# A norm's sums one unit later, single PSUM tiles at the start and in the last attention output, and seven products in one more column group

## The chip, the cores and the metric

One core of a Trainium2 chip runs the whole program in one launch. The metric is the device time of that launch in microseconds; the kernel before has a median of 2023.74 us in the three runs shown (2023.49 to 2025.34). The engines are TensorE (PE, with its weight loads PEld), VectorE (DVE), ScalarE (ACT), GpSimd (POOL) and SyncE (SP, which issues most transfers).

## The reference

A decoder of two layers over 256 tokens of width 2048. Layer 0 mixes by causal pooling, layer 1 by attention with keys and values computed from the stream after layer 0; each is followed by a gated FFN with a causal convolution. Every addition is followed by a layer norm.

```python
def layer_norm(x, g, b):
    mu = jnp.mean(xf, axis=-1, keepdims=True)
    var = jnp.mean(jnp.square(xf - mu), axis=-1, keepdims=True)
    y = (xf - mu) * lax.rsqrt(var + LN_EPS) * g + b
...
    for i in range(DEPTH):
        if i < N_A_LAYERS:
            mix = pool_mixer(h, pool_w_in[i], pool_w_grp[i], pool_scale[i], pool_w_out[i])
        else:
            if i == N_A_LAYERS:
                k_shared = (h @ shared_w_k).reshape(B_, S, N_HEADS, HEAD_DIM)
                v_shared = (h @ shared_w_v).reshape(B_, S, N_HEADS, HEAD_DIM)
            mix = dilated_attention(h, k_shared, v_shared, attn_w_q[j], attn_w_o[j])
        h = layer_norm(DEEPNORM_ALPHA * h + mix, ln1_g[i], ln1_b[i])
        ff = conv_ffn(h, ffn_w_up[i], ffn_conv_w[i], ffn_conv_b[i], ffn_w_down[i])
        h = layer_norm(DEEPNORM_ALPHA * h + ff, ln2_g[i], ln2_b[i])
    return h
```

## The kernel before

**Units.** All matrix products are cut into units: a block of 512 weight rows by 512 columns, loaded as one tile `raw`. A unit's float32 weights are split into a high part `wh` (cast by ACT, L99) and a low part `wl` (the rest, by DVE, L100), and three products of high and low parts stand for one float32 product. `run_units` walks through the list of units. For unit i it first calls `ahead(i)`, which issues loads up to five units on and splits up to three units on (`SP_AHEAD`); `wh` and `wl` have four buffers each, `raw` has three. Then come the functions that were put in `before[i]`, the unit's matmuls, then the functions in `pending` whose count has run out, and last the unit's own `post`. `later(n, fn)` puts a function in `pending`, to run n units on. Each engine carries out its instructions strictly in the order in which this walk writes them.

**Activations.** The stream stands transposed in four quarters `H[0..3]` (128 partitions x 4 x 256 tokens), with high and low parts for the matmuls in `XC[q]` (and in `XP[q]`, the stream scaled by the norm's gain but not yet normed). The start transposes x with TensorE into PSUM tiles `xT` (`x_quad`, L535 on): ACT casts the high part into XC, DVE subtracts for the low part, and ACT copies the float32 into H. PSUM has four tiles of two banks; `bank` gives one bank of such a tile, `pair` both.

**The norm.** `add_last` is the last product of a half layer. Behind its four column groups, `resid_last` adds the result to H, squares it, and folds it into the sums `S` and `Q`. `shift` first takes the mean of quarter 0 from all quarters, for quarters 1 to 3 of a second half layer (`first` false) by GpSimd transfers that accumulate (`less`, L409). `chain` (L428) lets TensorE sum S and Q over the partitions (L429, L430), and from these ACT and DVE make the reciprocal deviation and the mean; then come, a unit apart each, `norm(q)` (DVE, L443 and L444), `affine(q)` (ACT, L450, and the cast L452) and `lo(q)` (DVE, L305: the low part of XC[q]).

The first product after a norm does not wait for it: it uses XP and is corrected when it is evacuated (`norm_evac`, L474 to L478). After layer 0's FFN these are the four units of K for head group 0, called k0 to k3 here. The next four, q0 to q3, are Q for the same heads; q0 is the first to read XC[0], q3 the first to read XC[3]. Then come the units of V.

**Seven products.** Some units of the FFN's second product (`group_tm`, `mk_seven`) make a two by two block product with seven products of half size instead of eight; `sevens` says in which column groups. Such a unit is split in two, "a" and "b", and DVE forms sums of weight blocks for them (`split_sums`, L113 to L124). Quarters 0 to 6 of the first FFN do so in all four column groups, quarter 7 in two.

**Attention outputs.** `outputs(hq, ms)` multiplies the transposed weights with V for two heads at a time into one pair of banks; ACT casts the high part (L1119), DVE makes the low part (L1120). The product with `attn_w_o` follows, whose last unit of a column group reads these.

Of the kernel before, what the change touches and what calls it, by code (L numbers as in the profile page):

```python
# [9 lines left out]
F32 = mybir.dt.float32  # L10
# [3 lines left out]
OP = mybir.AluOpType  # L14
# [3 lines left out]
T = 256  # L18
P = 128
# [13 lines left out]
def trunk(ctx: ExitStack, tc: tile.TileContext, x, pool_w_in, pool_w_grp, pool_scale, pool_w_out,  # L33
# [3 lines left out]
    V, A, PE = nc.vector, nc.scalar, nc.tensor  # L37
# [10 lines left out]
    def pair(nm):  # L48
        return psp.tile([P, 2, 512], F32, name=nm, tag="ps")

    def bank(nm):
        return pair(nm)[:, 0, :]

    def pairs(ps, n=4):
        return [(m, min(2, n - m), ps[m].both) for m in range(0, n, 2)]
# [16 lines left out]
    pending, before = [], {}  # L72
# [62 lines left out]
    def later(n, fn):  # L135
        if n == 0:
            fn()
        else:
            pending.append([n, fn])
# [158 lines left out]
    def w4(nm):  # L298
        return lnp.tile([P, 4, T], F32, name=nm, tag="w4")

    def quad_tile(nm):
        return xcp.tile([P, 4, 2, XW], F32R, name=nm, tag="xc")

    def lo_part(dst, src, n):
        V.tensor_tensor(dst[:, 0:n, 1, :T], src, dst[:, 0:n, 0, :T].bitcast(F32), OP.subtract)  # L305
# [9 lines left out]
    H, XC, XP, ST = {}, {}, {}, {}  # L315
    vec, cvec, gbx = [], [], {}
    ident = const.tile([P, P], F32, name="ident")
# [13 lines left out]
    def resid_last(c, first, lay, which, after):  # L331
        def post(ps):
            for m, n, p in pairs(ps):
                y = H[c][:, m:m + n, :]
                if first and c == 0:
                    V.scalar_tensor_tensor(y, y, ALPHA, p[:, :, :T], op0=OP.mult, op1=OP.add)
                else:
                    V.tensor_tensor(y, y, p[:, :, :T], OP.add)
                if c < 3:
                    V.tensor_tensor(y, y, p[:, :, T:], OP.add)  # L340
                else:
                    square(3, m)
            if c == 0:
                ST["w4"] = w4("fold")
                s = fold(H[0], None, "S0", F32R)
                later(1, lambda: shift(s, first, lay, which))
            elif c < 3:
                n = 3 if c == 1 and not first else 1
                later(n, lambda: stats(c))
                later(n + 1, lambda: xp(c, lay, which))  # L350
            else:
                folds(3)
                xp(3, lay, which)
                later(1, lambda: chain(ps[0], lay, which, after))
        return post

    def square(q, m):
        if m == 0:
            ST["sq"] = lnp.tile([P, 4, T], F32, name="sq", tag="sq")
        A.activation(ST["sq"][:, m:m + 2], H[q][:, m:m + 2], AF.Square)  # L360
# [12 lines left out]
    def folds(q):  # L373
        ST["S"] = fold(H[q], ST["S"], "S")
        ST["Q"] = fold(ST["sq"], ST["Q"], "Q")

    def stats(q):
        square(q, 0)
        square(q, 2)
        folds(q)  # L380

    def shift(s, first, lay, which):
        ps = bank("shift")
        PE.matmul(ps[:, :T], ones4, s, start=True, stop=True)
        if first:
            cs = ST["w4"][:, 3:4, :]
        else:
            cs = pools["ffn"].tile([P, 2, T], F32, name="cs", tag="xs", bufs=1)[:, 0:1, :]
        A.activation(cs[:, 0, :], ps[:, :T], AF.Copy, scale=-1.0)
        cb = cs.to_broadcast([P, 4, T])  # L390
        ST["S"] = ST["Q"] = None

        def one():
            V.tensor_tensor(H[0], H[0], cb, OP.add)
            if first:
                pre(1)
            stats(0)

        def two():
            xp(0, lay, which)  # L400
            if first:
                pre(2)
                pre(3)

        def pre(q):
            V.scalar_tensor_tensor(H[q], H[q], ALPHA, cb, op0=OP.mult, op1=OP.add)

        def less(q):
            nc.gpsimd.dma_start(H[q], cb, accum_op=OP.add)  # L409

        later(1, one)
        later(2, two)
        if not first:
            for q in (1, 2, 3):
                less(q)

    def xp(q, lay, which):
# [10 lines left out]
    def chain(ps, lay, which, after):  # L428
        PE.matmul(ps[:, :T], onesd, ST["S"], start=True, stop=True)  # L429
        PE.matmul(ps[:, T:], onesd, ST["Q"], start=True, stop=True)  # L430
        rm = lnp.tile([P, 4, T], F32, name="rm", tag="sq")
        rs, mr, var = rm[:, 0, :], rm[:, 1, :], rm[:, 2, :]
        ST["rs"], ST["mr"] = rm[:, 0:1, :], mr
        A.activation(rm[:, 3, :], ps[:, :T], AF.Square)
        V.tensor_tensor(var, ps[:, T:], rm[:, 3, :], OP.subtract)
        A.activation(var, var, AF.Sqrt, bias=epst)
        V.reciprocal(rs, var)
        V.tensor_tensor(mr, ps[:, :T], rs, OP.mult)
        mb, rb = rm[:, 1:2, :].to_broadcast([P, 4, T]), rm[:, 0:1, :].to_broadcast([P, 4, T])
        g0 = 32 * which  # L440

        def norm(q):
            V.tensor_tensor(H[q], H[q], rb, OP.mult)  # L443
            V.tensor_tensor(H[q], H[q], mb, OP.subtract)  # L444

        def affine(q):
            XC[q] = quad_tile("xc")
            for m in range(4):
                j = 4 * q + m
                A.activation(H[q][:, m, :], H[q][:, m, :], AF.Identity,  # L450
                             scale=vec[lay][:, g0 + j:g0 + j + 1], bias=vec[lay][:, g0 + 16 + j:g0 + 17 + j])
            A.copy(XC[q][:, :, 0, :T], H[q])  # L452

        def lo(q):
            lo_part(XC[q], H[q], 4)
            if after is not None:
                later((8, 11, 14, 17)[q], lambda: after(q))

        norm(0)
        for q in range(4):  # L460
            if q > 0:
                later(1 + q, lambda q=q: lo(q - 1))
            later(1 + q, lambda q=q: affine(q))
            if q < 3:
                later(1 + q, lambda q=q: norm(q + 1))
        later(5, lambda: lo(3))
# [69 lines left out]
    def x_quad(q, halves=(0, 1)):  # L536
        xin = XIN
        if halves[0] == 0:
            H[q] = hp.tile([P, 4, T], F32, name="h", tag="h")
            XC[q] = quad_tile("xc")  # L540
        if halves[0] == 0:
            ST["xT"] = pair("xT")
        both = ST["xT"]
        for half in halves:
            for kk in range(2):
                for t in range(2):
                    k = 2 * half + kk
                    PE.transpose(both[:, half, kk * T + t * P:kk * T + t * P + P], xin[q, t][:, k * P:(k + 1) * P],
                                 ident)
        for half in halves:  # L550
            pv2 = both[:, half, :].rearrange("p (k t) -> p k t", k=2)
            s = slice(2 * half, 2 * half + 2)
            A.copy(XC[q][:, s, 0, :T], pv2)
            V.tensor_tensor(XC[q][:, s, 1, :T], pv2, XC[q][:, s, 0, :T].bitcast(F32), OP.subtract)
        if halves[-1] == 1:
            before.setdefault(min(q + 1, 3), []).append(
                lambda: A.copy(H[q], both.rearrange("p b (k t) -> p (b k) t", k=2)))

    def add_in(g, mids=()):
        group(pool_w_in[0], rows4, 512 * g, 512, xsrcs, pool_post(g), mode="a" if g == 3 else "ab", mids=mids)  # L560
# [1 line left out]
    def add_grp(g):  # L562
# [12 lines left out]
             True, 0, 0, after=lambda q: to_tokens(q))  # L575
# [8 lines left out]
    def ffn(lay):  # L584
# [5 lines left out]
        sevens = {q: every for q in range(8)}  # L590
        sets = {0: "C", 1: "A", 2: "B", 3: "C", 4: "A", 5: "B", 6: "A", 7: "CB"[lay], 9: "A"}
        if lay == 1:
            sevens[9] = (0, 2)
        else:
            sevens[7] = (0, 1)
        free, done = {}, {}

        def pads():
# [175 lines left out]
        for n in (0, 1):  # L774
            d = down(n, False)
            q = chunks[n + 1][0]
# [187 lines left out]
    qk, pr, oq, pT, vts = {}, {}, {}, {}, {}  # L964
# [140 lines left out]
    def outputs(hq, ms):  # L1105
        if ms[0] == 0:
            oq[hq] = quad_tile("o")
        vt = vts[hq]
        both = pair("o")
        for m in ms:  # L1110
            hd = slice(m * P, (m + 1) * P)
            ps = both[:, m % 2, :]
            t = pT.pop((hq, m))
            PE.matmul(ps[:, :T], vt[:, 0, hd], t[:, :T], start=True, stop=False)  # L1114
            PE.matmul(ps[:, P:T], vt[:, 1, hd], t[:, T:], start=False, stop=True)
        o = oq[hq][:, ms[0]:ms[0] + 2]
        for at in (slice(0, 1), slice(1, 2)) if hq == 3 else (slice(0, 2),):
            hi = o[:, at, 0, :T]
            A.copy(hi, both[:, at, :T])  # L1119
            V.tensor_tensor(o[:, at, 1, :T], both[:, at, :T], hi.bitcast(F32), OP.subtract)  # L1120

    def v_group(hq):
        js = (0, 1, 2, 3)
# [18 lines left out]
    with tc.tile_pool(name="start", bufs=1) as stp:  # L1142
        one1 = stp.tile([P, P], F32, name="one1")
        for q in range(NQ):
            for t in range(2):
                XIN[q, t] = stp.tile([P, 512], F32, name=f"xin{q}{t}")
            halves = [slice(0, 256), slice(256, 512)] if q == 0 else [slice(0, 512)]
# [130 lines left out]
```

## Time and profile before

| | us | share of the span |
|---|---|---|
| profiled execution | 2024.98 | |
| its span | 2023.2 | |
| PE busy | 2011.6 | 99% |
| DVE busy | 1728.5 | 85% |
| ACT busy | 1269.2 | 63% |
| POOL busy | 94.3 | 5% |
| granted clock of TensorE, mean | 0.999 | |

In the profile's rows the columns of a timeline are: start in us, duration, engine, line, operation, output<-input, shape, count, and in brackets the engine's idle time before the row with what ended it. A list of waits has: engine, tile and line that waited <- who was waited for: us in total, times, longest. A row of windows has: stretch, its length, busy time of PE, PEld, DVE, ACT and POOL with counts, the granted TensorE clock, the share of the DMA engines, GB/s. Matmuls overlap: what counts is the distance of their starts, not their duration.

### The profile page before, as it was taken

To read this page: it belongs to the slowest core of one execution; us is meant where nothing else is said; L and a number is where in the kernel's file an instruction comes from. 1 tells how busy PE (TensorE), PEld (TensorE's weight loads), DVE (VectorE), ACT (ScalarE), POOL (GpSimd) and SP (SyncE) were. 2 spreads that over 40 slices of the span, in tenths; PEclk is the share of its full clock that TensorE was granted. 3 is DMA by queue.
4 is the path that set the end of the run, shared out by engine and by line. 5 is a ranking of instruction groups with operands and counts; after the bars stand their busy time and mean duration, and the time that the engine had idled before them with its cause. 6 is when DMAs were issued, how large, how long until landed. Compare 5 with 4: busy or idle time off the path is not lost.

```text
span 2023.2 us, 31428 instructions
## 1 busy us (share of the span) xinstructions
PE 2011.6 (99%) x12742; PEld 1813.7 (90%) x12742; DVE 1728.5 (85%) x1822; ACT 1269.2 (63%) x1546; POOL 94.3 (5%) x154
## 2 busy tenths in 40 slices
PE   9999999999999999999999999999999999999999
PEld 8898988999899988888898988998899989989987
DVE  6868887999899999779796878787899899989898
ACT  5454686766766676656554444477767677667672
POOL 2000000000000000000000021000000000000000
PEclk9999999999999999999999999999999999999999
DMA  8565576676666767885565656557666757666765
GB/s 256 192 211 188 164 216 191 180 221 222 197 198 205 233 190 219 236 226 187 177 207 165 199 175 207 188 175 221 167 215 203 227 179 227 193 222 189 211 220 173
DMA packets 271825, 408.30 MB, mean 202 GB/s; under 512 B 74446, under 2 KB 86116, under 8 KB 271424
## 3 DMA queue, kind: packets, MB, share of 16 engines
q1 hardware_dynamic: 259488, 388.93, 59.1%
q0 software_dynamic: 11760, 16.70, 5.5%
q8 instruction: 100, 1.64, 0.3%
q10 hardware_dynamic: 432, 0.66, 0.1%
q14 instruction: 45, 0.37, 0.1%
HBM read 380.01 MB, written 2.10 MB: 189 GB/s over the span
## 4 chain that ended last, share of the span: by engine, by line
PE 98%; DVE 1%; DMA 0%; issue 0%; ACT 0%; SPq 0%; DVEq 0%
PE acc L180 44%; PE acc L181 22%; PE s L246 3%; PE s L244 3%; PE s L245 3%; PE acc L185 3%; PE t L246 2%; PE t L244 2%; PE t L245 2%; PE acc L184 2%; PE acc L183 2%; PE t L255 2%; PE t L257 2%; PE t L256 2%; PE s L1064 0%; PE o L1114 0%
## 5 line engine op out<-in xcount | busy, mean ns | idle before, releaser
L180 PE MATMUL acc<-xc,wh 128*128 128x512 f32 x3264 | 1151.8, 396 | 0.0
L181 PE MATMUL acc<-xc,wl 128*128 128x256 f32 x3264 | 916.0, 281 | 0.0
L100 DVE TENSOR_TENSOR wl<-raw,wh 128x2048 fp32r<-128x2048 f32 (+2 forms) x305 | 657.1, 2163 | 174.9 <-ACT wh L99 170.3
L180 PEld LDWEIGHTS acc<-xc,wh 128*128 128x128 f32 x3264 | 616.0, 189 | 143.3
L99 ACT CAST wh<-raw 128x2048 fp32r<-128x2048 f32 (+2 forms) x305 | 548.7, 1805 | 170.1 <-PE acc L180 70.4
L181 PEld LDWEIGHTS acc<-xc,wl 128*128 128x128 f32 x3264 | 615.4, 189 | 0.1
L113 ACT CAST wh<-raw 128x1024 fp32r<-128x1024 f32 x142 | 148.4, 1052 | 194.5 <-DVE raw L122 175.3
L114 DVE TENSOR_TENSOR wl<-raw,wh 128x1024 fp32r<-128x1024 f32 x142 | 169.4, 1221 | 11.2 <-ACT wh L113 11.2
L121 DVE TENSOR_TENSOR wl<-raw,wh 128x1536 fp32r<-128x1536 f32 x71 | 124.5, 1754 | 6.7 <-ACT wh L119 5.7
L119 ACT CAST wh<-raw 128x1536 fp32r<-128x1536 f32 x71 | 104.9, 1477 | 35.4 <-PE acc L180 28.2
L287 POOL DMA_DIRECT2D ht<-w x48 | 41.3, 1014 | 1446.7 <-DVE ht L877 722.1
L246 PE MATMUL t<-wh,g 128*128 128x256 f32 x376 | 105.7, 281 | 0.0
L244 PE MATMUL t<-wh,g 128*128 128x256 f32 x376 | 105.6, 281 | 0.0
L245 PE MATMUL t<-wl,g 128*128 128x256 f32 x376 | 105.4, 280 | 0.0
L620 ACT ACTIVATE c<-u,cv 128x256 f32<-128x256 f32 x172 | 89.5, 592 | 23.1 <-DVE f L682 16.6
L246 PE MATMUL s<-wh,xs 128*128 128x256 f32 x344 | 96.2, 280 | 0.0
L244 PE MATMUL s<-wh,xs 128*128 128x256 f32 x344 | 96.1, 279 | 0.0
L245 PE MATMUL s<-wl,xs 128*128 128x256 f32 x344 | 96.0, 279 | 0.0
L124 DVE TENSOR_TENSOR raw<-raw 128x1024 f32<-128x1024 f32 x71 | 87.0, 1225 | 2.4
L625 ACT ACTIVATE a<-u,cv 128x256 f32<-128x256 f32 x172 | 73.4, 499 | 11.9 <-DVE g L692 11.9
L611 ACT COPY u<-acc 128x512 f32<-128x512 f32 x84 | 46.9, 573 | 47.4 <-PE acc L181 47.1
L625 ACT ACTIVATE u<-u,cv 128x256 f32<-128x256 f32 x172 | 73.4, 499 | 0.0
(337 smaller groups left out, 3445.2 us busy)
## 6 DMA issues: line engine op xcount, KB each, us to landing
raw<-in_ffn_w_up_dram SPq DMA_DIRECT2D x160, 1024.0 KB, 5.2
raw<-in_ffn_w_down_dram SPq DMA_DIRECT2D x80, 1024.0 KB, 5.2
raw<-in_pool_w_out_dram SPq DMA_DIRECT2D x16, 1024.0 KB, 5.0
raw<-in_shared_w_k_dram SPq DMA_DIRECT2D x16, 1024.0 KB, 5.1
raw<-in_attn_w_q_dram SPq DMA_DIRECT2D x16, 1024.0 KB, 5.1
raw<-in_shared_w_v_dram SPq DMA_DIRECT2D x16, 1024.0 KB, 5.2
raw<-in_attn_w_o_dram SPq DMA_DIRECT2D x16, 1024.0 KB, 5.4
ht<-w POOLq DMA_DIRECT2D x50, 256.0 KB, 5.3
```

Of the source, the lines that this page charges most:

```text
L99: A.copy(wh[i][:, s], r[:, s])
L100: V.tensor_tensor(wl[i][:, s], r[:, s], wh[i][:, s].bitcast(F32), OP.subtract)
L113: A.copy(h[:, :, n], r[:, :, n])
L114: V.tensor_tensor(l[:, :, n], r[:, :, n], h[:, :, n].bitcast(F32), OP.subtract)
L119: A.copy(hs, rs)
L121: V.tensor_tensor(ls, rs, hs.bitcast(F32), OP.subtract)
L180: PE.matmul(ps[m].ap, h[:, k, c], q[:, k, :, :T], start=st, stop=False)
L181: PE.matmul(ps[m][:, :T], l[:, k, c], q[:, k, 0, :T], start=False, stop=sp)
L244: PE.matmul(to, xh, h[:, k, n], start=opens and kk == 0, stop=False)
L245: PE.matmul(to, xh, l[:, k, n], start=False, stop=False)
L246: PE.matmul(to, xl, h[:, k, n], start=False, stop=ends and kk == 1)
L625: A.activation(to[:, m, :], u[:, m, i:i + T], AF.Copy, scale=cv[:, i, j:j + 1])
```

## The change

The diff, with the call of the norm's sums first. The count of `chain` becomes 2 behind a second half layer, so that the sums stand behind k1 instead of k0; H[1] gets its shift from DVE instead of GpSimd. `x_quad` takes a PSUM tile for each half, makes the casts of a half right behind its transposes, and copies H at the start of unit q instead of the next. Quarter 7 of the first FFN takes seven products in column group 2 as well, where plain ones stood (24 matmuls of 512 columns become 42 of 256). The last two heads get a tile each in `outputs`, and the two before them one cast instead of two.

```diff
@@ resid_last
                 folds(3)
                 xp(3, lay, which)
-                later(1, lambda: chain(ps[0], lay, which, after))
+                later(1 if first else 2, lambda: chain(ps[0], lay, which, after))
@@ shift
             V.tensor_tensor(H[0], H[0], cb, OP.add)
             if first:
                 pre(1)
+            else:
+                V.tensor_tensor(H[1], H[1], cb, OP.add)
             stats(0)
...
         if not first:
-            for q in (1, 2, 3):
+            for q in (2, 3):
                 less(q)
@@ x_quad
-        if halves[0] == 0:
-            ST["xT"] = pair("xT")
-        both = ST["xT"]
         for half in halves:
+            ps = bank("xT")
             for kk in range(2):
                 for t in range(2):
                     k = 2 * half + kk
-                    PE.transpose(both[:, half, kk * T + t * P:kk * T + t * P + P], xin[q, t][:, k * P:(k + 1) * P],
-                                 ident)
-        for half in halves:
-            pv2 = both[:, half, :].rearrange("p (k t) -> p k t", k=2)
+                    PE.transpose(ps[:, kk * T + t * P:kk * T + t * P + P], xin[q, t][:, k * P:(k + 1) * P], ident)
+            pv2 = ps.rearrange("p (k t) -> p k t", k=2)
             s = slice(2 * half, 2 * half + 2)
             A.copy(XC[q][:, s, 0, :T], pv2)
             V.tensor_tensor(XC[q][:, s, 1, :T], pv2, XC[q][:, s, 0, :T].bitcast(F32), OP.subtract)
-        if halves[-1] == 1:
-            before.setdefault(min(q + 1, 3), []).append(
-                lambda: A.copy(H[q], both.rearrange("p b (k t) -> p (b k) t", k=2)))
+            before.setdefault(q, []).append(lambda s=s, pv2=pv2: A.copy(H[q][:, s, :], pv2))
@@ ffn
-            sevens[7] = (0, 1)
+            sevens[7] = (0, 1, 2)
@@ outputs
-        both = pair("o")
+        last = hq == 3 and ms[0] == 2
+        both = None if last else pair("o")
         for m in ms:
             hd = slice(m * P, (m + 1) * P)
-            ps = both[:, m % 2, :]
+            ps = bank("o") if last else both[:, m % 2, :]
...
+            if last:
+                hi = oq[hq][:, m, 0, :T]
+                A.copy(hi, ps[:, :T])
+                V.tensor_tensor(oq[hq][:, m, 1, :T], ps[:, :T], hi.bitcast(F32), OP.subtract)
-        o = oq[hq][:, ms[0]:ms[0] + 2]
-        for at in (slice(0, 1), slice(1, 2)) if hq == 3 else (slice(0, 2),):
-            hi = o[:, at, 0, :T]
-            A.copy(hi, both[:, at, :T])
-            V.tensor_tensor(o[:, at, 1, :T], both[:, at, :T], hi.bitcast(F32), OP.subtract)
+        if not last:
+            o = oq[hq][:, ms[0]:ms[0] + 2]
+            A.copy(o[:, :, 0, :T], both[:, :, :T])
+            V.tensor_tensor(o[:, :, 1, :T], both[:, :, :T], o[:, :, 0, :T].bitcast(F32), OP.subtract)
```

How this moves instructions is seen in three places. Lines of the changed kernel differ by two to four behind the first edit; a number behind `wl` is that of the unit. In the kernel before, k0 to k3 are units 198 to 201, q0 to q3 202 to 205, and V begins with 206; in the changed one all are one higher, since the added seven-product unit counts as two.

DVE, from the sums of the norm behind layer 0's FFN to the low part of XC[0] (L305). Before:

```order
L100 TENSOR_TENSOR wl201_8859<-raw201_8725,wh201_8858 128x2048
L435 TENSOR_TENSOR rm_8914<-acc_8656,rm_8914 128x256
L437 RECIPROCAL rm_8914<-rm_8914 128x256
L438 TENSOR_TENSOR rm_8914<-acc_8656,rm_8914 128x256
L443 TENSOR_TENSOR h_7393<-h_7393,rm_8914 128x1024
L444 TENSOR_TENSOR h_7393<-h_7393,rm_8914 128x1024
L100 TENSOR_TENSOR wl202_8925<-raw202_8789,wh202_8924 128x2048
L443 TENSOR_TENSOR h_7713<-h_7713,rm_8914 128x1024
L444 TENSOR_TENSOR h_7713<-h_7713,rm_8914 128x1024
L100 TENSOR_TENSOR wl203_8987<-raw203_8856,wh203_8986 128x2048
L305 TENSOR_TENSOR xc_8976<-h_7393,xc_8976 128x4x256
```

and now:

```order
L100 TENSOR_TENSOR wl202_8894<-raw202_8760,wh202_8893 128x2048
L100 TENSOR_TENSOR wl203_8950<-raw203_8824,wh203_8949 128x2048
L437 TENSOR_TENSOR rm_9003<-acc_8691,rm_9003 128x256
L439 RECIPROCAL rm_9003<-rm_9003 128x256
L440 TENSOR_TENSOR rm_9003<-acc_8691,rm_9003 128x256
L445 TENSOR_TENSOR h_7401<-h_7401,rm_9003 128x1024
L446 TENSOR_TENSOR h_7401<-h_7401,rm_9003 128x1024
L100 TENSOR_TENSOR wl204_9014<-raw204_8891,wh204_9013 128x2048
L445 TENSOR_TENSOR h_7722<-h_7722,rm_9003 128x1024
L446 TENSOR_TENSOR h_7722<-h_7722,rm_9003 128x1024
L100 TENSOR_TENSOR wl205_9076<-raw205_8947,wh205_9075 128x2048
L305 TENSOR_TENSOR xc_9065<-h_7401,xc_9065 128x4x256
```

One more weight split (q0's) stands ahead of the norm's first instruction; behind it the rows are the same as before, with the splits of q1 and q2 in place of those of q0 and q1.

DVE, some 15 us further on, at the low part of XC[3] (the second L305 before, the last row now) and the evacuation of K (tile `k`). Before:

```order
L100 TENSOR_TENSOR wl205_9113<-raw205_8984,wh205_9112 128x2048
L305 TENSOR_TENSOR xc_9102<-h_7975,xc_9102 128x4x256
L100 TENSOR_TENSOR wl206_9160<-raw206_9047,wh206_9159 128x2048
L305 TENSOR_TENSOR xc_9151<-h_8234,xc_9151 128x4x256
L474 TENSOR_TENSOR k_9196<-acc_8862,rm_8914 128x512
L477 SCALAR_TENSOR_TENSOR k_9196<-rm_8914,wgb_9197,k_9196 128x256 x2
L474 TENSOR_TENSOR k_9196<-acc_8863,rm_8914 128x512
```

and now:

```order
L100 TENSOR_TENSOR wl207_9188<-raw207_9073,wh207_9187 128x2048
L305 TENSOR_TENSOR xc_9177<-h_8010,xc_9177 128x4x256
L476 TENSOR_TENSOR k_9230<-acc_8897,rm_9003 128x512
L479 SCALAR_TENSOR_TENSOR k_9230<-rm_9003,wgb_9231,k_9230 128x256 x2
L476 TENSOR_TENSOR k_9230<-acc_8898,rm_9003 128x512
L479 SCALAR_TENSOR_TENSOR k_9230<-rm_9003,wgb_9231,k_9230 128x256 x2
L100 TENSOR_TENSOR wl208_9247<-raw208_9136,wh208_9246 128x2048
L305 TENSOR_TENSOR xc_9224<-h_8269,xc_9224 128x4x256
```

The low part of XC[3] has moved behind the evacuation of K and the split of the second V unit (208).

ACT at the start of the program, the casts of quarters 0 and 1 and the copies to H. Before:

```order
L553 CAST xc_153<-xT_154 128x2x256
L99 CAST wh0_173<-raw0_93 128x512 x3
L553 CAST xc_216<-xT_217 128x2x256 x2
L99 CAST wh1_256<-raw1_115 128x512 x4
L557 COPY h_152<-xT_154 128x1024
```

and now:

```order
L551 CAST xc_153<-xT_177 128x2x256
L99 CAST wh0_173<-raw0_93 128x512 x3
L553 COPY h_152<-xT_154 128x512
L553 COPY h_152<-xT_177 128x512
L551 CAST xc_219<-xT_220 128x2x256
L551 CAST xc_219<-xT_227 128x2x256
L99 CAST wh1_260<-raw1_115 128x512 x4
```

The copies to H stand ahead of the next quarter's casts instead of behind its weight casts, and each half has its own tile `xT`.

## The prediction

> **What bounds the kernel now.** I read the page's totals first, then TensorE's list of waits, then the stretches in which TensorE stands still, in order of time.
>
> ```profile
> span 2023.2 us, 31428 instructions
> PE 2011.6 (99%) x12742; PEld 1813.7 (90%) x12742; DVE 1728.5 (85%) x1822; ACT 1269.2 (63%) x1546; POOL 94.3 (5%) x154
> ...
> PE acc L429 <- DVE S L370: 2.6, 1, 2.6
> ```
>
> TensorE (PE) is busy 99% of the span, so time is gained only by fewer matmul columns or by filling the few holes. The largest is one place, the sums of the norm behind the first FFN. It looks like this, a TensorE timeline and a granted-clock window:
>
> ```profile
> 930.38 0.28 PE L185 MATMUL acc<-xp,wl 128*128 128x258 f32 x1
> 933.27 0.70 PE L429 MATMUL acc<-S,onesd 128*128 128x256 f32 x2 [2.61 <-DVE S L370]
> 934.78 1.22 PE L430 MATMUL acc<-Q,onesd 128*128 128x256 f32 x2 [0.82 <-DVE Q L370]
> ...
> 942.64 0.28 PE L183 MATMUL acc<-xp,wh 128*128 128x258 f32 x1
> 948.43 0.28 PE L183 MATMUL acc<-xp,wh 128*128 128x258 f32 x1
> ...
> 954.18 0.39 PE L180 MATMUL acc<-xc,wh 128*128 128x512 f32 x1
> ...
> 933.20:938.00 4.80, 3.91 (x15) 3.33 (x16) 4.73 (x9) 4.19 (x6) 0.00 (x0) 0.67 0.34 130
> ```
>
> The first K unit (k0) ends at 930.50, the sums wait for VectorE (DVE), and after the wait the clock is 0.67 over 4.8 us, which takes 4.8 x 0.33 = 1.6 us more. k2 starts at 942.64, k3 at 948.43 and the first Q unit (q0), the first that reads the normed XC[0], at 954.18: a unit is 5.75.
>
> **Part 1, the sums one unit later (with H[1] on DVE).** The wait at the old place goes away. DVE also loses a stall earlier, since H[1] no longer comes by an accumulating DMA:
>
> ```profile
> 901.48 0.69 DVE L338 TENSOR_TENSOR h<-h,acc 128x512 f32<-128x512 f32 x1 [4.73 <-DMA h<-cs]
> ```
>
> 4.7 us of idling become one 128x1024 add, at most 1.3 us as the L305 rows below, so DVE has S ready some 3.4 us earlier, near 929.8. I count no gain from that: what decides now is how late the norm itself gets. The norm behind layer 0's first add has the same instructions and no wait, so it measures the path from the sums to XC[0]'s low part, the last thing q0 needs:
>
> ```profile
> 224.15 0.60 PE L429 MATMUL acc<-S,onesd 128*128 128x256 f32 x2
> 227.45 1.75 DVE L437 RECIPROCAL rm<-rm 128x256 f32<-128x256 f32 x1 [0.91 <-ACT rm L436]
> ...
> 239.31 1.22 DVE L305 TENSOR_TENSOR xc<-h,xc 128x1024 fp32r<-128x1024 f32 x1
> ...
> 242.28 0.40 PE L180 MATMUL acc<-xc,wh 128*128 128x512 f32 x1
> ...
> 951.29 1.22 DVE L305 TENSOR_TENSOR xc<-h,xc 128x1024 fp32r<-128x1024 f32 x1
> ```
>
> From the sums (224.15) to the end of the low part (239.31 + 1.22 = 240.53) it takes 16.4 us; TensorE comes to the unit that reads it after 18.1 us, three units on. The DVE rows of the order shown ahead are the same in number after the sums now as there (two weight splits and norm(1) before the low part), and the path starts with ACT's square root, not with a queue, so 16.4 holds. But only two units are left to cover it: 18.1 - 5.75 = 12.4. **TensorE will stand 4.0 us before q0.** From k0's end q0 came after 954.18 - 930.50 = 23.7; now after 18.1 + 4.0 = 22.1: a gain of 1.6, which the half clock behind such a wait (1.6 as above) takes back.
>
> A second wait follows before q3, which reads XC[3]. Its low part has moved behind the evacuation of K and behind one weight split more. The rows of before for these links, DVE and ACT timelines, and TensorE's q2 and q3:
>
> ```profile
> 963.74 1.90 ACT L99 CAST wh<-raw 128x2048 fp32r<-128x2048 f32 x1
> ...
> 960.55 2.28 DVE L100 TENSOR_TENSOR wl<-raw,wh 128x2048 fp32r<-128x2048 f32 x1
> 967.88 1.22 DVE L305 TENSOR_TENSOR xc<-h,xc 128x1024 fp32r<-128x1024 f32 x1
> 969.02 0.68 DVE L474 TENSOR_TENSOR k<-acc,rm 128x512 f32<-128x512 f32 x1
> ...
> 971.83 0.91 ACT L478 ACTIVATE k<-k,wgb 128x256 f32<-128x256 f32 x2 [0.61 <-DVE k L477]
> ...
> 965.42 0.40 PE L180 MATMUL acc<-xc,wh 128*128 128x512 f32 x1
> ...
> 971.07 0.39 PE L180 MATMUL acc<-xc,wh 128*128 128x512 f32 x1
> ```
>
> There are four weight buffers, so the split of the first V unit, which reuses q0's, waits for the end of q0. From there, all in one chain: cast 1.9, split 2.2, low part of XC[2] 1.2, K's evacuation 969.02 to 972.74 = 3.7, cast of the second V unit 1.9, split 2.2, low part of XC[3] 1.2: 14.3 us. TensorE needs two units, 2 x 5.65 = 11.3 (q2 at 965.42, q3 at 971.07). **So it stands 3.0 to 3.1 us again before q3.** In before that low part ran at 967.88, ahead of K's evacuation, and nobody waited.
>
> Sum of part 1: -1.6 + 1.6 + 3.1 = +3.1, and up to +1.6 more if the clock falls a second time; I take half of that, +3.9. Ends: +1.5 (the clock never falls) to +4.7.
>
> The Trainium skill's page "TensorE: Matmul & The Clock Gate" (Part 1: The HAM clock gate) says that the clock halves after an idle window of about 3.4 us and returns after as long a busy one. Taken strictly, the second wait would never trip it and part 1 would be +3.1. The row above speaks against the strict reading: idle 2.61 and 0.82 with 0.70 of work between was enough.
>
> **Part 2, single PSUM tiles.** At the start, x_quad's second cast on ScalarE (ACT) waits for DVE's reading of the first half, because both lie in one tile; TensorE then waits for the split behind it.
>
> ```profile
> 12.66 0.59 ACT L553 CAST xc<-xT 128x512 fp32r<-128x512 f32 x1 [2.71 <-PE xT L548]
> 14.01 0.59 ACT L553 CAST xc<-xT 128x512 fp32r<-128x512 f32 x1 [0.76 <-DVE xc L554]
> ...
> 15.97 0.39 PE L185 MATMUL acc<-xc,wl 128*128 128x256 f32 x1 [0.29 <-DVE wl L100]
> ...
> 30.29 0.39 PE L185 MATMUL acc<-xc,wl 128*128 128x256 f32 x1 [0.35 <-DVE wl L100]
> ...
> 32.09 0.38 PE L185 MATMUL acc<-xc,wl 128*128 128x256 f32 x1
> ```
>
> With a tile for each half the first cast can start after four transposes instead of eight (0.45 us) and the second loses its 0.76. That is 1.2 us, more than the 0.45 that TensorE loses at the start of units 1, 2 and 3; in unit 3 three more steps take 32.09 - 30.29 = 1.8 instead of 3 x 0.36. Together 1.35 + 0.7 = 2.0 us gained. The copies of H, now two of 128x512 and a unit earlier, fit ACT's idle 2.71 us before 12.66. Ends: 0 (transposes wait for these copies, which now free the tiles) to -2.4.
>
> In outputs of the last head group the same wait stands between the two casts of o:
>
> ```profile
> 1235.64 0.37 ACT L1119 CAST o<-o 128x256 fp32r<-128x256 f32 x1 [0.49 <-DVE o L1120]
> ...
> 1235.66 0.50 PE L180 MATMUL acc<-o,wh 128*128 128x512 f32 x1 [0.23 <-DVE o L1120]
> 1235.99 0.28 PE L181 MATMUL acc<-o,wl 128*128 128x256 f32 x1
> 1236.52 0.50 PE L180 MATMUL acc<-o,wh 128*128 128x512 f32 x1 [0.24 <-DVE o L1120]
> ```
>
> At a pitch of 0.12 the matmul at 1236.52 was due at 1236.11, and the one before lost as much: 0.8 us, all of which the earlier cast covers. Ends 0 and -0.9. The merged casts of the first two heads have a whole unit before they are read.
>
> **Part 3, seven products for one column group more.** A plain unit and a seven-product unit of the same stage, by their first matmuls:
>
> ```profile
> 807.75 0.40 PE L255 MATMUL t<-wh,g 128*128 128x512 f32 x1
> ...
> 813.32 0.28 PE L244 MATMUL s<-wh,g 128*128 128x256 f32 x1
> ...
> 818.27 0.39 PE L180 MATMUL acc<-xc,wh 128*128 128x512 f32 x1
> ```
>
> 5.57 against 4.95: -0.6 us, once. DVE's work for a seven-product unit runs from 800.11 to 807.8, one transposition of 1.2 us among it, so 6.5 instead of the 2.2 of a plain split: 4.3 us more. What hides it is DVE's slack there:
>
> ```profile
> 800.11 0.69 DVE L120 TENSOR_TENSOR raw<-raw 128x512 f32<-128x512 f32 x1
> ...
> 805.53 2.31 DVE L114 TENSOR_TENSOR wl<-raw,wh 128x1024 fp32r<-128x1024 f32 x2
> ...
> 815.08 1.76 DVE L100 TENSOR_TENSOR wl<-raw,wh 128x1536 fp32r<-128x1536 f32 x1 [3.38 <-DMA h<-hb]
> ```
>
> Without that cover it would cost up to 4.3 - 3.4 = 0.9 us; two groups of this kind already run before it with no wait of TensorE. Ends -0.6 and +0.3.
>
> **Sum:** +3.9 - 2.0 - 0.8 - 0.6 = **+0.5 us**. The profiled execution took 2024.98 us, 1.8 around its span; the runs shown have a median of 2023.74, so I predict **2024.2 us**. A measurement of this kernel tells about 0.2%, 4 us, from no change. By the strict rule of the clock page the sum would be -0.3.
>
> **Rivals.** *The norm is in time* (faster): if the low parts were ready for q0 and q3, the whole loss of the old place would be won, 23.7 - 18.1 = 5.6, with parts 2 and 3 -9.0: 2014.8 us. For it: DVE is 3.4 us earlier. Against: the path starts only when TensorE reaches the sums. 15%.
> *The half clock holds two windows* (slower): each wait costs 3.2 instead of 1.6, from the point at which the matmuls after it are not dense enough to bring the clock back; part 1 is -1.6 + 3.1 + 6.4 = +7.9 and the sum +4.5: 2028.2 us. For it: the two waits lie within 30 us. Against: after 934.78 one window was enough. 18%.
> *The start gains nothing*, because transfers bound it:
>
> ```profile
> 15.00:22.00 7.00, 6.71 (x57) 6.51 (x57) 3.68 (x7) 4.06 (x8) 0.00 (x0) 1.00 1.04 383
> ```
>
> The DMA engines are full there (1.04). Then +2.5: 2026.2. Against: TensorE's waits name DVE. 12%. My forecast has the other 55%.
>
> Faster by over 0.2% is the first rival, 0.15; slower the second, 0.18; within, 0.67. The likeliest case alone spans 2021.5 to 2027; to hold the time 8 times in 10 I stretch it to 2018.5 to 2028.5.
>
> **What would show it.** Right: no wait of the sums for S or Q; TensorE waiting some 4 us for xc at the first Q unit and 3 us at the fourth, with a granted clock below 1 behind one or both; no waits for wl in the first 30 us; no second wait between o's casts. Wrong: no wait before q0, or waits for wl that stay.

## The result, and the profile after

The changed kernel takes 2028.63 us (median of 13 runs, 2025.82 to 2031.32) against 2024.23 us of the kernel before on the same chips (13 runs, 2021.59 to 2026.66): a ratio of 1.002, 95% interval 1.0013 to 1.0028. It is slower by 4.4 us, or 0.2%, and the interval excludes no change; the forecast was +0.5. The time is 0.1 us above the upper end of the forecast range (2028.5), but the kernel before is also 0.5 us slower here than in the runs from which the forecast started (2023.74). The profiled execution took 2029.02 us, 1.8 around its span.

The first line of the changed kernel's page, and below it its TensorE list of waits (total, times, longest):

```profile
span 2027.2 us, 31469 instructions
```

```profile
PE acc L180 <- DVE xc L305: 7.0, 2, 4.0
PE shift L384 <- DVE S L367: 2.3, 1, 2.3
```

The waits of the sums for S and Q (2.6 and 0.8) are gone, and so is the wait for o. In their place stand two waits for xc, 7.0 us together, which the forecast named, and one that it did not: 2.3 us for S at the matmul of the shift (line 384), some 45 us ahead of the sums. At the start the wait for wl fell from 0.9 to 0.2, but one of 0.9 for wh is new, and those for the tiles of x rose from 0.4 to 1.1.

The TensorE timeline of the changed kernel, at the ends of the stages ahead of the norm, the sums, q0, q1, q3, the first V unit and the end of outputs (start, duration, engine, line, then what it waited for):

```profile
40.46 0.23 PE L1196 MATMUL vT<-ident,vrow 80*128 80x80 f32 x1
...
860.12 0.40 PE L180 MATMUL acc<-g,wh 128*128 128x512 f32 x1
...
889.23 0.35 PE L384 MATMUL shift<-S,ones 128*128 128x256 f32 x1 [2.25 <-DVE S L367]
...
930.57 0.28 PE L183 MATMUL acc<-xp,wh 128*128 128x258 f32 x1
...
936.32 0.60 PE L431 MATMUL acc<-S,onesd 128*128 128x256 f32 x2
...
952.85 0.47 PE L180 MATMUL acc<-xc,wh 128*128 128x512 f32 x1 [3.95 <-DVE xc L305]
...
960.10 0.39 PE L180 MATMUL acc<-xc,wh 128*128 128x512 f32 x1
...
974.61 0.77 PE L180 MATMUL acc<-xc,wh 128*128 128x512 f32 x1 [3.02 <-DVE xc L305]
...
981.67 0.40 PE L255 MATMUL t<-wh,xc 128*128 128x512 f32 x1
...
1240.61 0.50 PE L180 MATMUL acc<-o,wh 128*128 128x512 f32 x1
```

The same places in the kernel before, as far as the prediction doesn't show them:

```profile
42.19 0.23 PE L1196 MATMUL vT<-ident,vrow 80*128 80x80 f32 x1
...
862.53 0.40 PE L180 MATMUL acc<-g,wh 128*128 128x512 f32 x1
...
889.23 0.28 PE L384 MATMUL shift<-S,ones 128*128 128x256 f32 x1
...
959.79 0.40 PE L180 MATMUL acc<-xc,wh 128*128 128x512 f32 x1
...
976.71 0.40 PE L255 MATMUL t<-wh,xc 128*128 128x512 f32 x1
```

Read as differences from place to place, they are the whole account of these two executions:

| step | forecast, us | profiled executions, us | from |
|---|---|---|---|
| start, single tiles | -2.0 | -1.73 | 42.19 to 40.46 |
| added sevens | -0.6 | -0.68 | 862.53 to 860.12, less the 1.73 |
| wait for S at the shift | 0 | +2.41 | 889.23 in both: the whole 2.41 won so far is gone |
| shift to the end of k0 | 0 | +0.07 | the first K unit ends at 930.50 and 930.57 |
| k0's end to q0 | -1.6 | -1.40 | 954.18 - 930.50 and 952.85 - 930.57 |
| q0 at half clock | +1.6 | +1.64 | 959.79 - 954.18 and 960.10 - 952.85 |
| wait before q3 | +3.1 | +3.23 | 971.07 - 959.79 and 974.61 - 960.10 |
| q3 at half clock | +0.8 | +1.42 | 976.71 - 971.07 and 981.67 - 974.61 |
| outputs, single tiles | -0.8 | -0.87 | 1236.52 - 976.71 and 1240.61 - 981.67 |
| sum | +0.5 | +4.1 | the spans differ by 4.0 |

VectorE of the changed kernel, where q0 and q3 get their low parts:

```profile
951.48 1.22 DVE L305 TENSOR_TENSOR xc<-h,xc 128x1024 fp32r<-128x1024 f32 x1
...
965.48 0.68 DVE L476 TENSOR_TENSOR k<-acc,rm 128x512 f32<-128x512 f32 x1
...
971.03 2.29 DVE L100 TENSOR_TENSOR wl<-raw,wh 128x2048 fp32r<-128x2048 f32 x1 [2.44 <-ACT wh L99]
973.24 1.22 DVE L305 TENSOR_TENSOR xc<-h,xc 128x1024 fp32r<-128x1024 f32 x1
```

From the sums (936.32) to the end of XC[0]'s low part (952.70) it takes 16.4 us, just what layer 0's first norm showed. XC[3]'s low part stands behind K's evacuation and the second V unit's split, as forecast. The granted clock in the two units behind the waits, from the changed kernel's stretches (the clock is the third number from the end):

```profile
952.85:956.95 4.10, 4.10 (x15) 3.53 (x16) 4.07 (x3) 3.07 (x5) 0.00 (x0) 0.60 0.69 248
974.61:977.45 2.84, 2.84 (x9) 2.46 (x10) 2.05 (x1) 0.00 (x0) 0.00 (x0) 0.50 0.90 323
```

0.40 of 4.10 us is 1.64, half of 2.84 is 1.42: behind both waits the clock was halved, once each.

### The profile page after: what moved, and what is told of

Its sections match the earlier page's. It is cut to its first block, busy times and chain, and to the rows that moved or that the text cites. A ratio compares the mean times of both kernels' runs of the same rounds, so it can differ in the third digit from the quotient of the medians.

```text
span 2027.2 us, 31469 instructions
## 1 busy us (share of the span) xinstructions
PE 2009.9 (99%) x12760; PEld 1813.2 (89%) x12760; DVE 1733.2 (85%) x1827; ACT 1270.7 (63%) x1551; POOL 93.1 (5%) x153
## 3 DMA queue, kind: packets, MB, share of 16 engines
q8 instruction: 100, 1.64, 0.3%
## 4 chain that ended last, share of the span: by engine, by line
PE 92%; DVE 3%; DMA 3%; ACT 2%; issue 1%; SPq 1%; DVEq 0%; ACTq 0%
PE acc L180 40%; PE acc L181 20%; PE s L246 3%; PE s L244 3%; PE s L245 3%; PE acc L184 3%; PE acc L185 3%; PE acc L183 3%; PE t L246 2%; PE t L244 2%; PE t L245 2%; PE t L255 2%; PE t L256 2%; PE t L257 2%; DVE wl L100 1%; DMA raw<-in_ffn_w_up_dram 1%
```

## Experiments

Each run is held against the runs of the kernel before on its own chip. A single profile is one draw: the kernel before alone scatters over spans from 2019 to 2025 us, so places in the timeline decide here, and medians where they can.

**The delay alone undone.** The changed kernel, with the sums back at their old place:

```
-                later(1 if first else 2, lambda: chain(ps[0], lay, which, after))
+                later(1, lambda: chain(ps[0], lay, which, after))
```

> The changed kernel with only the sums put back one unit earlier (H[1] stays on VectorE, single PSUM tiles and the added sevens stay). Theory: the loss sits in the delay alone, and H[1] on VectorE is a gain of its own. In the changed kernel S is ready at 929.66 and Q at 931.17 while k0 ends at 930.58, so at the old place the sums of S do not wait, those of Q wait at most 0.5 us, the clock does not halve, and the norm has three units again: no wait before q0 and q3. From the start of k1's old place to the end of q3 51.1 us become about 41.2: span 2027.2 - 9.9 = 2017.3 us. Rival: the wait for S comes back (2.6 us, with half a clock behind it 1.6) and only the two later waits go: 2021.5 us. Rival: xc is late here too, by over 1 us: above 2018.5.

2019.15 us (11 runs) against 2024.2; ratio 0.998, interval 0.9971 to 0.9989; span 2017.4. Its TensorE timeline at the sums, q0 and the first V unit:

```profile
930.46 0.60 PE L431 MATMUL acc<-S,onesd 128*128 128x256 f32 x2
...
948.97 0.48 PE L180 MATMUL acc<-xc,wh 128*128 128x512 f32 x1
...
971.82 0.40 PE L255 MATMUL t<-wh,xc 128*128 128x512 f32 x1
```

No bracket behind any row, and no wait for S or Q at the sums, nor for xc, in its list of waits: the norm keeps nobody waiting. From k0's end to V it takes 971.82 - 930.46 = 41.4 us, against 51.1 (981.67 - 930.57) with the delay. The delay costs 9.5 us by the medians (2028.63 - 2019.15), and with H[1] on VectorE the sums no longer need it.

**H[1] on VectorE alone**, in the kernel before:

```
             if first:
                 pre(1)
+            else:
+                V.tensor_tensor(H[1], H[1], cb, OP.add)
             stats(0)
...
-            for q in (1, 2, 3):
+            for q in (2, 3):
```

> The kernel before with only H[1]'s addition moved from the accumulating transfer to VectorE. Theory: the 2.6 us wait for S at the sums comes from that transfer. VectorE's stall of 4.73 us becomes one addition of 1.2, S is ready 3.4 us earlier, at about 929.8, before k0 ends at 930.5; Q's wait stays at most 0.5 and the clock does not halve: gain 2.6 + 0.4 + 1.6 = 4.6 us, span 2018.6 us. Rival: other work of VectorE fills the time and S stays where it was: 2023.2 us.

2020.41 us; ratio 0.9985, interval 0.9976 to 0.9993; span 2018.3. Its TensorE at the sums:

```profile
930.56 0.60 PE L431 MATMUL acc<-S,onesd 128*128 128x256 f32 x2
```

The wait for S, which the delay was to step around, came from the accumulating transfer, and this part removes it at its source: 3.8 us by the medians (2024.2 - 2020.41).

**The delay alone**, in the kernel before (H[1] still by transfer):

```
-                later(1, lambda: chain(ps[0], lay, which, after))
+                later(1 if first else 2, lambda: chain(ps[0], lay, which, after))
```

> The kernel before with only the sums one unit later (H[1] still by the accumulating transfer). Theory: VectorE has Q only at 934.7, then the xp work and two weight splits to about 940.7 before it can touch the norm, 2.9 us later than in the changed kernel: the wait before q0 is 4.0 + 2.9 = 6.9 us, the waits before q3 about 3, and the part costs 4.9 + 2.9 = 7.8 us: span 2031 us. Rival (the path of 16.4 us starts at the sums whatever lies ahead of it): the same 4.0 and 3.2 us as in the changed kernel, cost 4.9 us, span 2028.1 us.

2032.15 us (5 runs); ratio 1.0041, interval 1.0028 to 1.0053. The profiled execution is the fastest of the five, with a span of 2026.6; the spans reach 2032.9 us, the mean clocks 0.999 down to 0.996. Its TensorE:

```profile
952.84 0.77 PE L180 MATMUL acc<-xc,wh 128*128 128x512 f32 x1 [3.95 <-DVE xc L305]
...
974.44 0.47 PE L180 MATMUL acc<-xc,wh 128*128 128x512 f32 x1 [3.02 <-DVE xc L305]
```

The rival's waits, 3.95 and 3.02, are there to the hundredth: the 6.9 us that I expected are not. But the median span, 2030.4, is near the 2031 of my theory. None of the slower executions has a profile, so where they lose the other 4 us is not shown; their lower clocks point to more stretches at half clock. The next run shows one way to them.

**H[1] back on the transfer**, in the changed kernel (the inverse of the diff for H[1] above):

> The changed kernel with H[1]'s addition back on the accumulating transfer (the sums stay one unit later, single tiles and sevens stay). Theory: with the sums late, S is ready in time either way and the path of 16.4 us starts at the sums, so moving H[1] is worth nothing in this kernel: the waits of 4.0 and 3.2 us stay, span 2026 to 2029 us. Rival: VectorE's later end shows at the norm's first instruction and the wait before q0 grows to over 5.5 us: span 2029 to 2031 us.

2031.91 us (6 runs), ratio 1.0032, interval 1.002 to 1.0043; span 2031.1. VectorE first, then TensorE of this run with the stretch of q0 behind the wait; the last row is VectorE of the delay alone, at the place of the first:

```profile
901.84 0.69 DVE L338 TENSOR_TENSOR h<-h,acc 128x512 f32<-128x512 f32 x1 [4.48 <-DMA h<-cs]
...
941.00 0.42 DVE L435 TENSOR_TENSOR rm<-acc,rm 128x256 f32<-128x256 f32 x1
```

```profile
938.04 0.60 PE L429 MATMUL acc<-S,onesd 128*128 128x256 f32 x2
...
955.21 0.77 PE L180 MATMUL acc<-xc,wh 128*128 128x512 f32 x1 [4.60 <-DVE xc L305]
```

```profile
955.21:960.79 5.58, 5.58 (x17) 4.81 (x18) 5.55 (x5) 4.37 (x6) 0.00 (x0) 0.50 0.51 185
```

```profile
899.10 0.69 DVE L338 TENSOR_TENSOR h<-h,acc 128x512 f32<-128x512 f32 x1 [2.29 <-DMA h<-cs]
```

When the transfer lands late (4.48), the weight splits ahead of the norm end so late that its first instruction stands 941.00 - 938.04 = 3.0 us behind the sums, and the wait before q0 grows by 0.65 us. When it lands early (2.29), that instruction stands 1.9 us behind them (1.5 in the changed kernel) and the wait does not grow. So the path starts at the sums, with a small addition from what lies ahead, neither none nor 2.9. The longer wait had a second price: behind it the clock is 0.50 over 5.58 us, through two steps of 3.41 us instead of one (the last section shows these steps), which costs 1.2 us more than in the changed kernel. Another 1.4 of the 3.9 us that this profile's span is longer come from a half clock behind the wait at the shift (2.68 here). By the medians H[1] back on the transfer costs 3.3 us beside the delay (2031.91 - 2028.63), though the two intervals overlap.

**The start alone**, in the kernel before: the edit of x_quad from the diff, nothing else.

> The kernel before with only the single PSUM tiles at the start. Theory: the first full stage ends 1.7 to 2.1 us earlier (the first transposition of the vectors' row at 40.1 to 40.5 instead of 42.19), and without the added sevens nearly all of it reaches the shift's matmul: it starts at 887.2 to 888.0 instead of 889.23; span 1.2 to 2 us shorter for the same loss at the sums. Rival: transfers pace the end of the FFN, the shift stays at 889.0 to 889.3 and nothing is gained.

2022.0 us against 2024.02; ratio 0.9986, interval 0.9977 to 0.9995. TensorE at the vectors' row, the shift and the sums:

```profile
39.49 0.23 PE L1190 MATMUL vT<-ident,vrow 80*128 80x80 f32 x1
...
886.59 0.28 PE L384 MATMUL shift<-S,ones 128*128 128x256 f32 x1
...
929.89 0.70 PE L429 MATMUL acc<-S,onesd 128*128 128x256 f32 x2 [1.87 <-DVE S L370]
```

42.19 - 39.49 = 2.70 us at the start, and 889.23 - 886.59 = 2.64 of it reach the shift, with no wait there: transfers do not hold this stage back by themselves. At the sums 0.7 us more is won, since S is late by 1.87 instead of 2.61 there.

**The sevens alone**, in the kernel before:

```
-            sevens[7] = (0, 1)
+            sevens[7] = (0, 1, 2)
```

> The kernel before with only the added seven-product column group. Theory: it saves 0.68 us of TensorE but puts VectorE and the weight transfers behind it later, so that S for the shift is ready only near 889.1 as in the changed kernel; the shift's matmul starts at 889.1 to 889.3 instead of 888.55, the 0.68 us are waited away, span as before (its runs scatter from 2019 to 2024). Rival (the forecast): a gain of 0.6, shift at 888.6. Rival: a net loss, shift later than 889.8.

2022.21 us; ratio 0.9992, interval 0.9983 to 1.0001: not to be told from no change. TensorE at the shift:

```profile
889.97 0.36 PE L384 MATMUL shift<-S,ones 128*128 128x256 f32 x1 [1.29 <-DVE S L367]
```

TensorE comes there 0.7 us earlier and leaves 0.74 later than before. By this place it is the net loss of the third case, by a hair; the medians show no loss (2022.21 against 2024.02). The profile's span is 2020.0 for another reason: in this execution H[1]'s transfer kept VectorE 2.01 us instead of 4.73, and the sums of S found S ready.

**The sevens undone**, in the changed kernel and then in the one with the sums at their old place:

```
-            sevens[7] = (0, 1, 2)
+            sevens[7] = (0, 1)
```

> The changed kernel with the added seven-product column group taken out again. Theory: that group delays VectorE and the weight transfers behind it, and the new wait of 2.3 us for S before the matmul of the shift comes from it. Without it S is ready at 888.0 at the latest (as in the kernel before) and TensorE arrives at about 887.5: wait at most 0.5 us, span 2027.2 + 0.7 - 1.8 = 2026.1 us. Rival: transfers pace the end of the FFN whatever the group does, the shift stays at 889.2 and the span at 2027.2 us, with a wait of 1.7 us.

> The changed kernel with the sums one unit earlier and without the added sevens: what is left is H[1] on VectorE and the single PSUM tiles. Theory: the gains of both experiments add, no wait for xc, no half clock at the sums, no wait for S at the shift: the shift at 887.2 to 888 instead of 889.1, span 2017.4 - 1.1 to 1.9 = about 2016 us, fastest of all. Rival: the sevens' saving was worth as much as their wait, span 2017.4.

The first: 2027.01 us, ratio 1.0016 (1.0007 to 1.0025), span 2026.8, with no wait for S at the shift (888.76). In this execution the clock fell to 0.83 between 10 and 20 us, so the start gave only 0.65 us, which is why the shift comes later than expected. The second, with H[1] on VectorE and the single tiles alone, is the fastest kernel of all: 2017.6 us (5 runs, 2017.08 to 2018.88), ratio 0.9966, interval 0.9954 to 0.9979, span 2015.3. With the sevens the median is 1.5 us higher here (2019.15) and 1.6 us higher in the changed kernel; the intervals overlap both times, and the places decide. What SyncE issues around the added group, weight tiles (`raw`) and the transposed stream (`h<-hb`), without the sevens:

```profile
795.55 2.57 SPq L89 DMA_DIRECT2D raw<-in_ffn_w_up_dram  x2
803.17 3.86 SPq L821 DMA_DIRECT2D h<-hb  x6
807.12 0.55 SPq L89 DMA_DIRECT2D raw<-in_ffn_w_up_dram  x1
```

and with them; below it VectorE at the second split of a unit pair and at the transposition:

```profile
796.35 0.37 SPq L89 DMA_DIRECT2D raw<-in_ffn_w_up_dram  x1
804.10 3.86 SPq L821 DMA_DIRECT2D h<-hb  x6
808.06 0.55 SPq L89 DMA_DIRECT2D raw<-in_ffn_w_up_dram  x1
```

```profile
800.51 2.41 DVE L114 TENSOR_TENSOR wl<-raw,wh 128x1024 fp32r<-128x1024 f32 x2
802.84 1.24 DVE L831 STREAM_TRANSPOSE hb<-ht 128x1024 f32<-128x1024 f32 x1
```

The second weight tile is issued at 808.06 instead of before 798.2, some 10 us later, and in that time the share of the DMA engines between 800 and 810 falls from 0.57 to 0.34. In SyncE's queue this load has moved behind the six transfers of the stream. They wait for the transposition (802.84 + 1.24 = 804.08), and the load follows right behind the last of them. The code gives the reason: a seven-product pair counts as two units and its second half loads nothing, so `ahead`, which looks five units on, comes to the next tile one unit later. The pair also holds one of the three raw buffers until its second split ends, at 800.51 + 2.41 = 802.92; that explains 5 us of the 10 at most. No run separates the two causes. The transfers then stay behind (their share between 860 and 870 is 0.94, against 0.71 without the sevens), ACT gets a weight tile there at 862.91 instead of 857.71, and S is ready at 888.95 instead of 885.41.

**K's evacuation one unit later**, in the changed kernel:

```
-            later(2 if hq == 0 and nm == "k" else 0, lambda: evac(ps))
+            later(3 if hq == 0 and nm == "k" else 0, lambda: evac(ps))
```

> The changed kernel with the evacuation of K one unit later, so that the low part of XC[3] and the weight split before it come ahead of it on VectorE. Theory: the wait before q3 comes from that order. The chain from q1's end is then cast 1.9, split 2.2, low part 1.2 = 5.3 us against a unit of 5.7 before q3: the wait of 3.2 us and the half clock behind it (1.4) go, span 2027.2 - 4.6 = 2022.6 us, the wait before q0 stays 4.0. Rival: the evacuation of 3.7 us now stands ahead of the split for the second V unit and TensorE waits there instead, by up to 3 us: span 2025 to 2027 us.

2025.39 us; ratio 1.0004, interval 0.9996 to 1.0013; span 2024.1. VectorE, then TensorE at the start of q3:

```profile
971.45 1.22 DVE L305 TENSOR_TENSOR xc<-h,xc 128x1024 fp32r<-128x1024 f32 x1
```

```profile
972.92 0.40 PE L180 MATMUL acc<-xc,wh 128*128 128x512 f32 x1
```

The low part ends at 972.67, q3 starts without a wait, none appears at V, and the wait before q0 stays (3.9). The order on VectorE was the cause of the second wait. Some of the 4.6 us went back at the shift, whose wait was 3.0 here and halved the clock.

**The first wait filled.** 32 matmuls on the identity ahead of q0, in the bank that q0 then overwrites, and after that 17:

```
+                if state["done"] == 203:
+                    for _ in range(32):
+                        PE.matmul(ps[0][:, :P], ident, ident, start=True, stop=True)
```

> The changed kernel with 32 matmuls of 128x128 on the identity put into the bank of the first Q unit ahead of its first real matmul, which overwrites them: about 3.5 us of work in the first 4.1 us wait. Theory: the first Q unit takes 7.25 us instead of 5.65 because the wait halves the clock. With the wait filled it takes 5.6 to 5.8 us, while the wait for xc shrinks to about 0.6 and the unit starts at the same time behind the sums: span 2027.2 - 1.5 = 2025.7 us, the half clock before the third wait at q3 stays. Rival: the slow stretch has another cause, the unit stays at 7.2 us and the span at 2027 us. Rival: the added matmuls delay the unit: above 2027.5.

> The run with the filled wait again, with 17 matmuls on the identity instead of 32: each took two passes of 0.11 us, so 32 filled 7.1 us and pushed the first Q unit 3 us back. 17 fill 3.7 us of the 4.1. Theory: the first Q unit starts where it does without them, some 22.3 us behind the end of k0, and takes 5.7 us instead of 7.25: from k0's end to the start of the second Q unit 28.0 us instead of 29.5; span 2027.2 - 1.5 = 2025.7 us if nothing else moves (the wait at the shift scatters by 1 us and can trip the clock there too). Rival: the unit still takes 7.2 us.

The first was mis-sized: 32 took 7.1 us, two instructions each, and pushed q0 back (2031.32 us, ratio 1.0033, interval 1.0021 to 1.0044). The second, TensorE, and the stretch of q0:

```profile
934.89 0.28 PE L186 MATMUL acc<-xp,wh 128*128 128x258 f32 x1
...
953.05 3.96 PE L176 MATMUL acc<-ident 128*128 128x128 f32 x34
957.16 0.47 PE L183 MATMUL acc<-xc,wh 128*128 128x512 f32 x1 [0.15 <-DVE xc L308]
```

```profile
957.16:962.89 5.73, 5.73 (x32) 4.90 (x33) 5.70 (x5) 4.38 (x6) 0.00 (x0) 1.00 0.55 183
```

q0 starts 22.3 us behind k0's end (934.89), as without them, and takes 5.73 us at full clock instead of 7.25. The half clock comes from the wait. The total does not show the gain: 2029.39 us, ratio 1.0024 (1.0015 to 1.0033), against 2028.63 of the changed kernel. The profiled execution is the slowest of the eleven; in it the clock also fell to 0.83 between 10 and 20 us and to 0.76 for 7.2 us behind the shift. Why the median gained nothing stays open.

## Why the prediction was right, and where it was not

- **The sums.** Forecast: waits of 4.0 and 3.0 to 3.1 us before q0 and q3, xc the cause of both, half a clock behind. Measured 3.95 and 3.02; putting the sums back removes both, and moving K's evacuation removes the second alone. This step was right in mechanism and size.
- **The half clock.** I took half of the second one, +0.8; it came whole, +1.42, while the delay alone has the same wait of 3.02 without it: whether it comes is a matter of luck (last section). With that the part is +4.9 instead of +3.9, just above its upper end of 4.7. The rival "the half clock holds two windows" names nearly the right time, 2028.2, for the wrong reason: in the changed kernel each wait cost one window. What it feared can happen, though: behind the wait of 4.60, with H[1] back on the transfer, the clock was at half for two.
- **The start and outputs.** -1.73 and -0.87 against -2.0 and -0.8; the start alone gave -2.70. Right in mechanism and about in size. Of the nine profiled executions with the new start seven won 1.7 to 2.7 us by the vectors' row; in the other two the clock fell to 0.83 between 10 and 20 us, and one won 0.65 and one lost 0.2.
- **The sevens: the step that failed.** "What hides it is DVE's slack there" counted VectorE's time alone and looked for a wait behind the group itself. What the extra unit moved was a weight load: behind six other transfers in SyncE's queue, it started some 10 us late, and TensorE paid at the shift, 75 us on: +2.41 against the -0.68 won. Without the sevens this wait is gone in both kernels that were tried. The earlier start sharpens it (1.3 us of wait without it, 2.3 with it): TensorE runs ahead of transfers that do not. My bound of +0.3 was too low by 1.4 us.
- **H[1] on VectorE.** "I count no gain from that" was too little. Without the delay it is the best part of the change, 3.8 us, and it makes the delay needless. Beside the delay it still kept the wait before q0 at 3.95 instead of up to 4.60, and the clock at half for one window instead of two. That this part and the delay cure the same wait was not seen.

The rival "the norm is in time" falls: the path is 16.4 us whatever VectorE gains ahead of it. "The start gains nothing" falls as well, by the run with the start alone.

## What to carry to other kernels

When two edits cure one wait, price each without the other: here the one at the source is worth 4 us, and the one that steps around it then costs 9.5. A consumer may be moved back only as far as the work behind it has slack; count the units that are left to cover the longest path from it, and see what shares its queue. For a saving of TensorE columns ask also whether it changes the order in which transfers are issued and how long a buffer is held; the price is then paid where the transfers next bind, not where the edit stands.

## What was not expected of the hardware

**Equal waits, different clock.** Waits of 2.25 us at the shift left the clock whole, in the changed kernel and in the one with the sums put back; a wait of 2.29 us there, in the run with 17 filling matmuls, halved it, and so did those of 2.68, 2.95 and 3.28 us in three others. The wait of 3.02 before q3 halved it in the changed kernel and not in the delay alone. Within a trace the granted clock changes only at whole multiples of 3.41 us from its other changes (953.68, 957.10, 974.16 and 977.58 in the changed kernel). Cut along these steps, the stretches differ. The changed kernel at the wait before q3 and behind it, then at the shift:

```profile
970.75:974.16 3.41, 0.83 (x6) 0.47 (x4) 3.13 (x2) 2.15 (x2) 0.00 (x0) 1.00 0.00 0
974.16:977.58 3.42, 2.98 (x9) 2.62 (x10) 2.50 (x2) 0.00 (x0) 0.00 (x0) 0.50 0.85 289
```

```profile
885.43:888.84 3.41, 1.54 (x10) 1.10 (x8) 3.27 (x6) 1.39 (x1) 0.00 (x0) 1.00 0.75 253
```

Now the delay alone at the wait before q3, and the run with 17 filling matmuls at the shift:

```profile
969.55:972.96 3.41, 1.87 (x11) 1.35 (x10) 2.10 (x1) 2.90 (x2) 0.00 (x0) 1.00 0.00 0
972.96:976.37 3.41, 1.93 (x11) 1.74 (x12) 3.41 (x3) 0.28 (x1) 0.00 (x0) 1.00 0.58 165
```

```profile
889.00:892.41 3.41, 1.12 (x7) 0.74 (x7) 3.31 (x6) 0.50 (x2) 0.00 (x0) 1.00 0.90 308
```

In the changed kernel the wait of 3.02 leaves TensorE idle for 2.58 us of one step (3.41 - 0.83), and the next is at half clock. In the delay alone the same wait straddles two steps, idle for 1.54 and 1.48 us, and the clock stays. At the shift 1.87 us of one step idle did nothing, 2.29 us halved the next. So in these pairs it counts how a wait falls on the steps, and these lie differently in each execution. The boundary is not sharp: in the start alone 1.68 us (929.03 to 932.43, at the sums) were enough. The Trainium skill's page "TensorE: Matmul & The Clock Gate" (Part 1: The HAM clock gate) says that the window runs freely and does not start with the work, and gives it as about 3.4 us; the steps here agree. Its idle window, read as one that is idle throughout, does not agree with the 2.29 us.

**The accumulating transfer scatters.** VectorE's wait for the same transfer was 2.0, 2.3, 4.0, 4.5 and 4.7 us in the profiles of five kernels. Two of these, the kernel before (4.73) and the delay alone (2.29), have the same instructions up to there. A loss that hangs on this transfer can show in one profile and not in the next.
